# Seven products for eight in three block pairs of a decoder's FFN input product

## The chip, the cores and the metric

One Trainium2 chip, one of its cores. The metric is the device time of one execution in microseconds (us); lower is better. Of several runs the median counts.

## What is computed

Two decoder layers over 256 tokens of width 1024, all in float32. A layer has a combined input projection, a sparse and a differential attention, gated up projections and an output projection; then comes the feed forward, which the change is about:

```
h = rms_norm(x, ffn_norm)
gate, up = jnp.split(h @ w_ffn_in, 2, axis=-1)      # 1024 -> 2 x 2816
x = x + (jax.nn.silu(gate) * up) @ w_ffn_out        # 2816 -> 1024
```

## The kernel before, in words

Every float32 operand of a dense product is split into a high part, rounded to the type that TensorE multiplies in one pass, and the low rest. `mm3` (lines 170 to 174) makes three matmuls of each product: high x high, high x low (of the weight), low (of the activation) x high. The activations (128 tokens x 128 of K) are the stationary operand, up to 512 columns of weights the moving one.

Weights come in units of 1 MB, 512 of K x 512 columns (or 256 of K x 1024 for the output product), in the order of `unit_order` (lines 55 to 69). A unit is loaded in two halves of 128x1024 into a ring of eight buffers (`load_half`, line 112, tag `raw`, issued on SyncE's queue) and split half by half (`split_half`): ScalarE copies the high part (line 135), VectorE subtracts for the low part (line 136). High and low parts lie in rings of four units (tags `wh`, `wl`), so that a unit's split waits until the product of the unit four places ahead is done.

TensorE and GpSimd keep the order in which the program is written. That of VectorE, ScalarE and the loads is found by a planner. `tick` counts blocks of TensorE's work, and `later` sets steps to run some ticks on.

The feed forward (lines 785 to 852) has eleven slabs of 256 gate and 256 up columns. `slab(s, t)` makes the input product of token tile t with one slab: 8 blocks of K x 3 matmuls of 512 columns into one bank of PSUM, from two units (`fi`). `fi_fin` (line 792) applies Silu on ScalarE (line 794), multiplies by up on VectorE (line 795), and three ticks later transposes the hidden tile and splits it (`hilo`, lines 212 and 213). `fo_part` (line 807) makes the output product of a slab's hidden tiles, 6 matmuls per token tile and half of the columns, into four banks (`facc`) that are held through the feed forward (line 813); the eight banks of PSUM share one tag (line 97). From slab 1 on the output product of the slab before follows each slab; those of the last three (`TAIL`) stand at the end, token tile by token tile. Between them the next layer's norm begins: sum (line 819), square (line 230), reciprocal root on GpSimd (lines 208 and 209), scaling (line 242), transposes (`norm_T`, line 244).

Before the feed forward the norm of the first token tile is transposed ahead of the last block of the output projection (line 772), that of the second in the middle of `slab(1, 0)` (line 825).

Of the kernel before, what the change touches and what calls it, by code (L numbers as in the profile page):

```python
# [10 lines left out]
F32 = mybir.dt.float32  # L11
# [3 lines left out]
ALU = mybir.AluOpType  # L15
# [10 lines left out]
TAIL = 3  # L26
# [16 lines left out]
RAWS = 8  # L43
# [5 lines left out]
MT_AT, FI_AT = 3, 3  # L49
WO = ((0, 0, 0), (0, 1, 0), (0, 0, 1), (1, 0, 0), (1, 1, 0), (0, 1, 1), (1, 0, 1), (1, 1, 1))  # L50
FRONT = ("gA0", "ix")
# [3 lines left out]
def unit_order():  # L55
    o = []

    def blk(n):
        o.extend([(n, 0), (n, 1)])

    for n in FRONT + BLOCKS:
        blk(n)
    o.extend([("wo", i) for i in range(4)])
    for s in range(NFO):
        blk(f"fi{s}")
        if 0 < s <= NFO - TAIL:
            o.append(("fo", s - 1))
    o.extend([("fo", s) for s in range(NFO - TAIL, NFO)])
    return o
# [3 lines left out]
PACKED = [u for u in ORDER if u[0] != "ix"]  # L73
# [3 lines left out]
def tile_trunk(ctx, tc, x, positions, wpk, widx, gnorm, gbias, gqk, dlam, subln, const, invf, out):  # L77
# [22 lines left out]
    seq, uidx = [], {}  # L100
    for l in range(DEPTH):
        n = 0
        for nm in ORDER:
            uidx[(l,) + nm] = len(seq)
            if nm[0] == "ix":
                seq.append((widx[l, nm[1]], 2 * IDXW))
            else:
                seq.append((wpk[l, n], 1024))
                n += 1
    ready, raws, loaded, split = [], {}, [0], [0]  # L110

    def load_half():
        n = loaded[0]
        loaded[0] += 1
        i, j = divmod(n, 2)
        src, w = seq[i]
        raws[n] = wp.tile([P, 1024], F32, name=f"raw{i}{j}", tag="raw", bufs=RAWS)[:, :w]
        nc.sync.dma_start(raws[n], src[j])

    def split_half(parts=1, between=None):  # L120
        n = split[0]
        split[0] += 1
        i, j = divmod(n, 2)
        w = seq[i][1]
        if j == 0:
            ready.append([wp.tile([P, 2048], F32R, name=f"w{h}{i}", tag="w" + h, bufs=RING) for h in "hl"])
        hi, lo = ready[i]
        if n not in raws:
            load_half()
        raw = raws.pop(n)  # L130
        m = w // parts
        for k in range(parts):
            c = slice(j * w + k * m, j * w + (k + 1) * m)
            piece = raw[:, k * m:(k + 1) * m]
            nc.scalar.activation(hi[:, c], piece, AF.Copy)  # L135
            nc.vector.tensor_tensor(lo[:, c], piece, hi[:, c].bitcast(F32), ALU.subtract)  # L136
            if k == 0 and between:
                between()
# [4 lines left out]

    def unit(l, name, i, kc, w):
# [25 lines left out]
    def mm3(acc, stat, mov, first, last):  # L170
        (sh, sl), (mh, ml) = stat, mov
        nc.tensor.matmul(acc, lhsT=sh, rhs=mh, start=first, stop=False)  # L172
        nc.tensor.matmul(acc, lhsT=sh, rhs=ml, start=False, stop=False)  # L173
        nc.tensor.matmul(acc, lhsT=sl, rhs=mh, start=False, stop=last)  # L174
# [40 lines left out]
    def heads(v, n):  # L215
        return v.rearrange("p (h d) -> p h d", h=n)
# [27 lines left out]
    def norm_T(N, t, *gs):  # L244
        for g in gs or range(2):
            b = bank(f"{N['name']}T{t}{g}")
            transposes(b, N["h"][t, g], range(4))
            hilo(*[a[:, 4 * g:4 * g + 4, t * P:(t + 1) * P] for a in N["T"]], heads(b, 4))

# [21 lines left out]
    for _ in range(8):  # L271
        load_half()
# [390 lines left out]
    for l in range(DEPTH):  # L663
# [34 lines left out]
        def y_tiles(n):  # L698
            return [pp.tile([P, 4, S], F32R, name=f"{n}{h}{l}", tag="yT", bufs=2) for h in "hl"]
# [91 lines left out]

        def fi_fin(s, t, acc):
# [4 lines left out]
            def fin():  # L797
                b = bank(f"aTT{l}{s}{t}")
                transposes(b, g, range(2, 4))
                a = t2k([P, 2, 2, P], f"aT{l}{s}{t}", F32R)  # L800
                hilo(a[:, 0], a[:, 1], heads(b[:, :S], 2))
                aT[s, t] = a
            later(FI_AT, fin)
# [3 lines left out]
        def fo_part(s, t, c, a=0, b=512):  # L807
# [6 lines left out]
            for kc in range(2):  # L814
                mm3(facc[t, c][:, a:b], [aT[s, t][:, j, kc] for j in range(2)],
                    [w[:, kc, 512 * c + a:512 * c + b] for w in W], first and kc == 0, end and kc == 1)
# [38 lines left out]
def pack(w_in, w_up_a, w_up_b, w_out, w_ffn_in, w_ffn_out):  # L855
# [8 lines left out]
    for l in range(DEPTH):  # L864
        for h in range(2):
            widx[l, h] = lay(w_in[l, 512 * h:512 * h + 512, IDX:IDX + IDXW])
        for n, (name, i) in enumerate(PACKED):
# [4 lines left out]
            elif name == "wo":  # L872
                c, k = divmod(i, 2)
                w = w_out[l, 512 * k:512 * k + 512, 512 * c:512 * c + 512]
            elif name.startswith("fi"):
# [40 lines left out]
```

## Time and profile before

| | |
|---|---|
| median of 3 runs | 781.02 us (780.72 to 781.04) |
| profiled execution | span 778.8 us; no other time of its own is shown |
| TensorE busy | 769.7 us (99%), 3718 instructions, transposes among them |
| VectorE busy | 502.6 us (65%) |
| ScalarE busy | 422.6 us (54%) |
| GpSimd busy | 80.5 us (10%) |
| moved by DMA | 137.83 MB, mean 177 GB/s |
| first layer's feed forward | from 207.4 us of the span on |

The span runs from the first to the last instruction. PE is TensorE, PEld its weight loads, DVE VectorE, ACT ScalarE, POOL GpSimd, SPq the queue of SyncE. Matmuls overlap, so that a busy time of PE says that it never stood idle, not that it ran at its peak. A wait is idle time of an engine with the line that it waited at and the instruction that ended the wait. The granted clock is that of TensorE, 1.00 being full speed.

### The profile page before, as it was taken

To read this page: it belongs to the slowest core of one execution; us is meant where nothing else is said; L and a number is where in the kernel's file an instruction comes from. 1 tells how busy PE (TensorE), PEld (TensorE's weight loads), DVE (VectorE), ACT (ScalarE), POOL (GpSimd) and SP (SyncE) were. 2 spreads that over 40 slices of the span, in tenths; PEclk is the share of its full clock that TensorE was granted. 3 is DMA by queue.
4 is the path that set the end of the run, shared out by engine and by line. 5 is a ranking of instruction groups with operands and counts; after the bars stand their busy time and mean duration, and the time that the engine had idled before them with its cause. 6 is when DMAs were issued, how large, how long until landed. Compare 5 with 4: busy or idle time off the path is not lost.

```text
span 778.8 us, 10446 instructions
## 1 busy us (share of the span) xinstructions
PE 769.7 (99%) x3718; PEld 631.6 (81%) x3718; DVE 502.6 (65%) x907; ACT 422.6 (54%) x922; POOL 80.5 (10%) x103
## 2 busy tenths in 40 slices
PE   8999999999999999999999999999999999999998
PEld 5877888888888888888888788788888888888887
DVE  4899767777764544455478986677766644554541
ACT  5776687565553433443357585876645534444440
POOL 6541220010110000000011310200001000000000
PEclk9999999999999999999999999999999999999999
DMA  8855645356546655556456365534564754566501
GB/s 290 298 170 172 220 159 176 113 162 202 193 149 227 204 189 189 162 186 197 146 176 216 124 202 152 187 122 151 187 189 163 242 189 163 179 199 204 175 0 55
DMA packets 41013, 137.83 MB, mean 177 GB/s; under 512 B 5201, under 2 KB 5969, under 8 KB 40962
## 3 DMA queue, kind: packets, MB, share of 16 engines
q1 hardware_dynamic: 40880, 136.97, 53.5%
q8 instruction: 29, 0.48, 0.2%
q0 software_dynamic: 80, 0.20, 0.1%
q14 instruction: 22, 0.18, 0.1%
q10 hardware_dynamic: 2, 0.00, 0.0%
HBM read 136.11 MB, written 1.05 MB: 176 GB/s over the span
## 4 chain that ended last, share of the span: by engine, by line
PE 88%; DVE 4%; ACT 3%; DMA 2%; POOL 1%; issue 1%; SPq 0%; ACTq 0%; DVEq 0%
PE fi L174 10%; PE fi L173 10%; PE fi L172 10%; PE fo L174 5%; PE fo L173 5%; PE fo L172 5%; PE gB L172 2%; PE gB L174 2%; PE wo L174 2%; PE wo L172 2%; PE gB L173 2%; PE wo L173 2%; PE gA L172 1%; DMA raw<-wpk 1%; PE gA L174 1%; PE gA L173 1%
## 5 line engine op out<-in xcount | busy, mean ns | idle before, releaser
L136 DVE TENSOR_TENSOR wl<-raw,wh 128x1024 fp32r<-128x1024 f32 (+2 forms) x254 | 299.4, 1205 | 129.5 <-ACT wh L135 128.7
L135 ACT ACTIVATE wh<-raw 128x1024 fp32r<-128x1024 f32 (+2 forms) x254 | 255.2, 1044 | 138.8 <-PE fo L174 50.0
L172 PE MATMUL fo<-wh,aT 128*128 128x512 f32 (+1 forms) x182 | 71.4, 392 | 0.0
L174 PE MATMUL fo<-wh,aT 128*128 128x512 f32 (+1 forms) x182 | 69.7, 383 | 0.0
L173 PE MATMUL fo<-wl,aT 128*128 128x512 f32 (+1 forms) x182 | 69.7, 383 | 0.0
L172 PE MATMUL fi<-wh,f0Th 128*128 128x512 f32 x176 | 69.6, 395 | 0.0
L172 PE MATMUL fi<-wh,f1Th 128*128 128x512 f32 x176 | 69.6, 395 | 0.0
L174 PE MATMUL fi<-wh,f1Tl 128*128 128x512 f32 x176 | 68.7, 390 | 0.0
L174 PE MATMUL fi<-wh,f0Tl 128*128 128x512 f32 x176 | 68.7, 390 | 0.0
L173 PE MATMUL fi<-wl,f0Th 128*128 128x512 f32 x176 | 68.6, 390 | 0.0
L173 PE MATMUL fi<-wl,f1Th 128*128 128x512 f32 x176 | 68.6, 390 | 0.0
L794 ACT ACTIVATE sg<-fi 128x256 f32<-128x256 f32 x44 | 16.9, 384 | 83.5 <-PE fi L174 83.5
L795 DVE TENSOR_TENSOR sg<-sg,fi 128x256 f32<-128x256 f32 x44 | 18.4, 418 | 43.5 <-ACT sg L794 43.5
L174 PEld LDWEIGHTS fo<-wh,aT 128*128 128x128 f32 x182 | 34.2, 188 | 6.7
L173 PEld LDWEIGHTS fo<-wl,aT 128*128 128x128 f32 x182 | 34.3, 188 | 6.0
L172 PEld LDWEIGHTS fo<-wh,aT 128*128 128x128 f32 x182 | 34.2, 188 | 6.0
L174 PEld LDWEIGHTS fi<-wh,f0Tl 128*128 128x128 f32 x176 | 33.0, 188 | 6.9
L174 PEld LDWEIGHTS fi<-wh,f1Tl 128*128 128x128 f32 x176 | 33.0, 188 | 6.9
L173 PEld LDWEIGHTS fi<-wl,f1Th 128*128 128x128 f32 x176 | 33.1, 188 | 6.5
L173 PEld LDWEIGHTS fi<-wl,f0Th 128*128 128x128 f32 x176 | 33.1, 188 | 6.5
L172 PEld LDWEIGHTS fi<-wh,f1Th 128*128 128x128 f32 x176 | 33.0, 188 | 6.5
L172 PEld LDWEIGHTS fi<-wh,f0Th 128*128 128x128 f32 x176 | 33.0, 188 | 6.5
(880 smaller groups left out, 1548.7 us busy)
## 6 DMA issues: line engine op xcount, KB each, us to landing
raw<-wpk SPq DMA_DIRECT2D x244, 512.0 KB, 4.4
raw<-widx SPq DMA_DIRECT2D x8, 324.0 KB, 6.8
x<-x SPq DMA_DIRECT2D x4, 256.0 KB, 3.7
gf<-gnorm SPq DMA_DIRECT2D x4, 256.0 KB, 5.7
out<-x SPq DMA_DIRECT2D x3, 256.0 KB, 2.0
ga<-gnorm SPq DMA_DIRECT2D x2, 256.0 KB, 4.3
gq<-gqk SPq DMA_DIRECT2D x2, 160.0 KB, 6.3
dl<-dlam SPq DMA_DIRECT2D x2, 128.0 KB, 5.1
```

The source lines that it names most:

```text
L135: nc.scalar.activation(hi[:, c], piece, AF.Copy)
L136: nc.vector.tensor_tensor(lo[:, c], piece, hi[:, c].bitcast(F32), ALU.subtract)
L172: nc.tensor.matmul(acc, lhsT=sh, rhs=mh, start=first, stop=False)
L173: nc.tensor.matmul(acc, lhsT=sh, rhs=ml, start=False, stop=False)
L174: nc.tensor.matmul(acc, lhsT=sl, rhs=mh, start=False, stop=last)
L794: nc.scalar.activation(g[:, :S], acc[:, :S], AF.Silu)
L795: nc.vector.tensor_tensor(g[:, S:], g[:, :S], acc[:, S:], ALU.mult)
```

## The change

Three pairs of slabs (3 and 4, 6 and 7, 9 and 10) get another input product. A pair has 512 gate and 512 up columns and K in two halves, so its weights are four units: 11 and 21 for gate (first and second half of K), 12 and 22 for up. Eight products of 128 tokens with one unit would be needed; token tile 0 and 1 have A11, A12 and A21, A22 as halves of K. Instead there are seven, with T1 = 12 - 11, T2 = 22 - T1, T3 = 22 - 12, T4 = 21 - T2 on the weights and S1 = A21 + A22, S2 = S1 - A11, S3 = A11 - A21, S4 = A12 - S2 on the activations: X = A11 x 11, Y = A12 x 21, V = S4 x 22, X += S2 x T2, Z = S3 x T3, X += S1 x T1, Z += A22 x T4. The gate of tile 0 is X + Y, its up X + V at the end; tile 1 has the later sums of X and Z.

The differences are made on VectorE, in the buffer of one of their operands (T1 in that of 11, T3 in that of 12, T4 in that of T2) but for T2, which has one of its own; 22 is loaded into the buffer of the attention outputs (tag `yT`). The splits are instructions of 128x2048 on VectorE, and on ScalarE for the T's. The sums S are made once per layer (`quarter_sums`) from the transposed norm. Loading buffers are four of 128x2048, in place of eight of 128x1024; a unit's two loads go to one buffer.

In the feed forward VectorE and ScalarE keep the written order now: behind product i come the high part of unit i+4, the low part of unit i+3 and the difference that unit i+5 needs. Dense slabs (0, 1, 2, 5, 8) use a unit for both token tiles, one after the other, before the next unit. The tail has two slabs. Core of the diff:

```diff
@@ -23,7 +23,7 @@
-TAIL = 3
+TAIL = 2
...
-RAWS = 8
+RAWS = 4
...
+QUAD_AT = (3, 3)
...
+FFN = (("D", 2), ("Q", 3), ("D", 5), ("Q", 6), ("D", 8), ("Q", 9))
+LOOK = 4
+PRODUCTS = ("11", "21", "22", "fo", "T2", "T3", "T1", "fo", "T4")
+LOADED = {"11": "11", "T1": "12", "21": "21", "22": "22"}
...
-    for s in range(NFO):
-        blk(f"fi{s}")
-        if 0 < s <= NFO - TAIL:
-            o.append(("fo", s - 1))
-    o.extend([("fo", s) for s in range(NFO - TAIL, NFO)])
+    blk("fi0")
+    blk("fi1")
+    done = 0
+    for kind, s in FFN:
+        for n in PRODUCTS if kind == "Q" else (0, 1, "fo") if done else (0, 1):
+            o.append((n, done) if n == "fo" else (("fi" if kind == "D" else "q") + str(s), n))
+            done += n == "fo"
+    o.extend([("fo", s) for s in range(done, NFO)])
...
+    def raw_of(u):
+        if u not in held:
+            src, w = where[u]
+            name = "raw" + "".join(str(a) for a in u)
+            if u[2] == "22":
+                raw = pp.tile([P, 2048], F32, name=name, tag="yT", bufs=1)
+            else:
+                raw = wp.tile([P, 2048], F32, name=name, tag="raw", bufs=RAWS)[:, :2 * w]
+            for j in range(2):
+                nc.sync.dma_start(raw[:, j * w:j * w + w], src[j])
+            held[u] = raw
+        return held[u]
...
+    def difference(n):
+        l, name, i = seq[n]
+        if n + 1 < len(seq) and seq[n + 1][2] == "T2":
+            l, name, i = seq[n + 1][:2] + ("T1",)
+        elif name[0] != "q" or i == "T1":
+            return
+        D = diffs.setdefault((l, name), {})
+        def less(new, a, b, to=None):
+            a, b = [D[x] if x[0] == "T" else raw_of((l, name, x)) for x in (a, b)]
+            to = {"a": a, "b": b}[to] if to else b8([P, 2048], f"T2{l}{name}")
+            nc.vector.tensor_tensor(to, a, b, ALU.subtract)
+            D[new] = to
+        if i == "T1":
+            less("T1", "12", "11", "b")
+        elif i == "T2":
+            less("T2", "22", "T1")
+        elif i == "T3":
+            less("T3", "22", "12", "b")
+        elif i == "T4":
+            less("T4", "21", "T2", "b")
+    def high(n):
+        u = seq[n]
+        raw = diffs[u[:2]].pop(u[2]) if u[2] in ("T1", "T3", "T4") else diffs[u[:2]]["T2"] if u[2] == "T2" else raw_of(u)
+        hi = new_ready(n)[0]
+        m = 1 if u[1][0] == "q" and u[2][0] == "T" else 2
+        w = 2048 // m
+        for k in range(m):
+            nc.scalar.activation(hi[:, k * w:k * w + w], raw[:, k * w:k * w + w], AF.Copy)
+        if u[2] == "11":
+            raw_of(u[:2] + ("21",)), raw_of(u[:2] + ("12",))
+        stage["raw", n] = raw
+    def low(n):
+        nc.vector.tensor_tensor(ready[n][1], stage.pop(("raw", n)), ready[n][0].bitcast(F32), ALU.subtract)
+        split[0] += 2
+    def staged(k, end):
+        for fn, m in ((high, k), (low, k - 1), (difference, k + 1)):
+            n = max(stage.get(fn, 0), split[0] // 2)
+            while n <= min(m, end):
+                fn(n)
+                n += 1
+            stage[fn] = n
...
+    def quarter_sums(N, banks):
+        name = N["name"]
+        f1, f2 = N["f"]
+        tiles = [b8([P, 4, 4, P], f"{name}S{h}", F32R) for h in "hl"]
+        N["S"] = [[a[:, i] for a in tiles] for i in range(4)]
+        s1, s2, s3, s4 = [t2k([P, 512], f"{name}s{i}") for i in range(4)]
+        nc.scalar.activation(s4, banks[1], AF.Copy)
+        nc.vector.tensor_tensor(s1, banks[0], s4, ALU.add)
+        nc.vector.tensor_tensor(s3, f1, banks[0], ALU.subtract)
+        nc.vector.tensor_tensor(s2, s1, f1, ALU.subtract)
+        nc.vector.tensor_tensor(s4, f2, s2, ALU.subtract)
+        for i, v in ((0, s1), (3, s4), (1, s2), (2, s3)):
+            hilo(*N["S"][i], heads(v, 4))
...
-                norm_T(NF, 0)
+                keep_quarters(NF, norm_T(NF, 0))
...
+        def ahead(name, i):
+            staged(uidx[l, name, i] + LOOK, uidx[l, "fo", NFO - 1])
+        def fo_all():
+            s = fo_next[0]
+            fo_next[0] += 1
+            for t in range(NT):
+                for c in range(2):
+                    fo_part(s, t, c)
+                tick()
+                if t == 0:
+                    ahead("fo", s)
+        def dense(s):
+            acc = [bank(f"fi{s}{l}{t}") for t in range(NT)]
+            for half in range(2):
+                for t in range(NT):
+                    by_tok(acc[t], fT, t, unit(l, f"fi{s}", half, 4, 512), 4 * half, 4, half == 0, half == 1)
+                    if half == 1:
+                        fi_fin(s, t, acc[t])
+                    tick()
+                ahead(f"fi{s}", half)
+        def quad(s):
+            name = f"{l}{s}"
+            def A(t, g):
+                return [a[:, 4 * g:4 * g + 4, t * P:(t + 1) * P] for a in fT]
+            S1, S2, S3, S4 = NF["S"]
+            def product(acc, stat, n, first, fins=()):
+                W = unit(l, f"q{s}", n, 4, 512)
+                for kc in range(4):
+                    mm3(acc, [a[:, kc, :] for a in stat], [w[:, kc, :] for w in W],
+                        first and kc == 0, kc == 3, not first)
+                for fin in fins:
+                    fin()
+                tick()
+                ahead(f"q{s}", n)
+            G, U = [[t2k([P, 512], f"{n}{t}{name}") for t in range(NT)] for n in "gu"]
+            def copied(to, p):
+                return lambda: nc.scalar.activation(to, p, AF.Copy)
+            def plus(to, p):
+                return lambda: nc.vector.tensor_tensor(to, to, p, ALU.add)
+            def added(to, a, p):
+                return lambda: nc.vector.tensor_tensor(to, a, p, ALU.add)
+            def silu(t):
+                return lambda: nc.scalar.activation(G[t], G[t], AF.Silu)
+            def gated(t):
+                def f():
+                    nc.vector.tensor_tensor(U[t], G[t], U[t], ALU.mult)
+                    later(QUAD_AT[t], lambda: hidden_T(s, t, U[t], range(4)))
+                return f
+            X = bank(f"qX{name}")
+            product(X, A(0, 0), "11", True, [copied(G[0], X)])
+            Y = bank(f"qY{name}")
+            product(Y, A(0, 1), "21", True, [plus(G[0], Y), silu(0)])
+            V = bank(f"qV{name}")
+            product(V, S4, "22", True)
+            fo_all()
+            product(X, S2, "T2", False, [copied(G[1], X)])
+            Z = bank(f"qZ{name}")
+            product(Z, S3, "T3", True)
+            product(X, S1, "T1", False, [copied(U[1], X), added(U[0], U[1], V), gated(0), plus(U[1], Z)])
+            fo_all()
+            product(Z, A(1, 1), "T4", False, [plus(G[1], Z), silu(1), gated(1)])
         slab(0, 0)
-        slab(1, 0, mid=lambda: norm_T(NF, 1))
-        for s in range(NFO):
-            for t in range(NT):
-                if s > 1 or t:
-                    slab(s, t)
-            if 0 < s <= NFO - TAIL:
-                for t in range(NT):
-                    for c in range(2):
-                        fo_part(s - 1, t, c)
-                    tick()
+        slab(1, 0, mid=lambda: quarter_sums(NF, norm_T(NF, 1)))
+        with tc.manual_schedule(engines={mybir.EngineType.DVE, mybir.EngineType.Activation}):
+            for i in range(2):
+                slab(i, 1, mid=lambda: ahead(f"fi{i}", 0))
+                ahead(f"fi{i}", 1)
+            for kind, s in FFN:
+                if kind == "Q":
+                    quad(s)
+                else:
+                    dense(s)
+                    if fo_next[0]:
+                        fo_all()
+            fo_all()
```

Not shown: the dictionary of loads by unit, `keep_quarters` (two ScalarE copies of A11 and A12's banks), `hidden_T` (transposes and splits two hidden blocks for a dense slab, four for a pair), and the packing of units 11, 12, 21, 22.

## Rows read from the trace of the kernel before

**Rows 1.** The page's head, engines' busy time, and the chain that ended last.

```profile
span 778.8 us, 10446 instructions
PE 769.7 (99%) x3718; PEld 631.6 (81%) x3718; DVE 502.6 (65%) x907; ACT 422.6 (54%) x922; POOL 80.5 (10%) x103
...
PE 88%; DVE 4%; ACT 3%; DMA 2%; POOL 1%; issue 1%; SPq 0%; ACTq 0%; DVEq 0%
```

**Rows 2.** Waits of PE: us in total, times, longest.

```profile
PE a0T L181 <- DVE a0h L242: 1.6, 1, 1.6
PE warm L279 <- DVE idle L274: 1.4, 1, 1.4
PE aq10T L181 <- DVE aq10q L367: 0.8, 1, 0.8
...
```

**Rows 3.** Busy time by stretch, the middle of layer 0's feed forward.

```profile
core 0: us, PE busy (x) PEld busy (x) DVE busy (x) ACT busy (x) POOL busy (x), PEclk, DMA share, GB/s
...
231.00:376.00 145.00, 145.00 (x657) 119.55 (x656) 73.34 (x88) 62.74 (x88) 0.00 (x0) 1.00 0.58 190
```

**Rows 4.** Timeline, PE in an output product and a hidden tile's transposes: start, duration.

```profile
300.03 0.39 PE L172 MATMUL fo<-wh,aT 128*128 128x512 f32 x1
...
303.20 0.39 PE L174 MATMUL fo<-wh,aT 128*128 128x512 f32 x1
...
303.44 0.38 PE L181 MATMUL aTT<-cst,sg 128*128 128x128 f32 x2
...
303.89 0.39 PE L173 MATMUL fi<-wl,f0Th 128*128 128x512 f32 x1
```

**Rows 5.** Groups by line and shape, VectorE's splits: busy us, mean ns.

```profile
L136 DVE TENSOR_TENSOR wl<-raw,wh 128x1024 fp32r<-128x1024 f32 x242 | 290.4, 1225 | 127.3 <-ACT wh L135 126.6
...
L136 DVE TENSOR_TENSOR wl<-raw,wh 128x648 fp32r<-128x648 f32 x8 | 6.3, 828 | 1.2 <-ACT wh L135 1.2
```

**Rows 6.** Timeline, DVE and ACT around the feed forward's start.

```profile
182.75 0.68 DVE L213 TENSOR_TENSOR mTl<-mT,mTh 128x512 fp32r<-128x512 f32 x1
183.35 1.22 DVE L136 TENSOR_TENSOR wl<-raw,wh 128x1024 fp32r<-128x1024 f32 x1
...
203.03 3.49 DVE L136 TENSOR_TENSOR wl<-raw,wh 128x1024 fp32r<-128x1024 f32 x3
...
223.38 2.36 DVE L136 TENSOR_TENSOR wl<-raw,wh 128x1024 fp32r<-128x1024 f32 x2 [2.88 <-ACT wh L135]
...
207.55 2.01 ACT L135 ACTIVATE wh<-raw 128x1024 fp32r<-128x1024 f32 x2 [0.64 <-PE wo L174]
```

**Rows 7.** Timeline, a slab's end handed from PE to ACT to DVE.

```profile
308.90 0.39 PE L174 MATMUL fi<-wh,f0Tl 128*128 128x512 f32 x1
...
309.32 0.38 ACT L794 ACTIVATE sg<-fi 128x256 f32<-128x256 f32 x1 [3.41 <-PE fi L174]
...
309.74 0.42 DVE L795 TENSOR_TENSOR sg<-sg,fi 128x256 f32<-128x256 f32 x1 [2.32 <-ACT sg L794]
```

**Rows 8.** Loads in 231 to 376 us: rate in 40 slices, landing, SPq's waits.

```profile
GB/s 269 374 268 131 75 257 250 271 23 163 276 234 198 8 279 292 181 113 131 238 220 269 14 197 293 211 167 15 285 283 205 86 139 268 199 262 7 220 251 1
...
DMA to landing us min/median/max: 3.1/4.2/6.0
...
SPq L118 <- DVE wl L136: 82.7, 34, 6.5
```

**Rows 9.** Timeline, the next layer's norm at the end of layer 0.

```profile
384.98 0.69 DVE L819 TENSOR_TENSOR x<-x,fo 128x512 f32<-128x512 f32 x1 [3.40 <-PE fo L174]
...
386.97 0.57 POOL L209 TENSOR_TENSOR a1r<-a1r,mhalf 128x1 f32<-128x1 f32 x1
...
387.58 1.42 DVE L242 SCALAR_TENSOR_TENSOR a1h<-x,a1r,ga 128x512 f32<-128x512 f32 x2 [1.54 <-POOL a1r L209]
...
390.48 1.03 PE L181 MATMUL a1T<-cst,a1h 128*128 128x128 f32 x8
```

More of the change, by code (lines that the diff above doesn't have):

```diff
@@ L97, in bank, with new_ready @@
         return ps.tile([P, 512], F32, name=name, tag="ps", bufs=8)
-    seq, uidx = [], {}
+    seq, uidx, where = [], {}, {}
     for l in range(DEPTH):
[L102 to L106, printed above, removed]
-            else:
[L108 to L118, printed above, removed]
+        for n, u in enumerate(PACKED):
+            where[(l,) + u] = (wpk[l, n], 1024)
+        for j in range(2):
+            where[l, "ix", j] = (widx[l, j], 2 * IDXW)
+        for u in ORDER:
+            uidx[(l,) + u] = len(seq)
+            seq.append((l,) + u)
+    held, ready, split = {}, [], [0]
+    def raw_of(u):
[4 more added lines that the diff above has]
+                raw = pp.tile([P, 2048], F32, name=name, tag="yT", bufs=1)
+            else:
+                raw = wp.tile([P, 2048], F32, name=name, tag="raw", bufs=RAWS)[:, :2 * w]
+            for j in range(2):
+                nc.sync.dma_start(raw[:, j * w:j * w + w], src[j])
+            held[u] = raw
+        return held[u]
+    def new_ready(i):
+        assert len(ready) == i
+        ready.append([wp.tile([P, 2048], F32R, name=f"w{h}{i}", tag="w" + h, bufs=RING) for h in "hl"])
+        return ready[i]
     def split_half(parts=1, between=None):
@@ L123, in split_half @@
         i, j = divmod(n, 2)
[L124 to L130, printed above, removed]
+        hi, lo = ready[i] if j else new_ready(i)
+        raw = raw_of(seq[i])
+        w = raw.shape[-1] // 2
         m = w // parts
@@ L168, in thread, with mm3 @@
             later(start + i, s)
-    def mm3(acc, stat, mov, first, last):
+    def mm3(acc, stat, mov, first, last, more=False):
         (sh, sl), (mh, ml) = stat, mov
-        nc.tensor.matmul(acc, lhsT=sh, rhs=mh, start=first, stop=False)
-        nc.tensor.matmul(acc, lhsT=sh, rhs=ml, start=False, stop=False)
-        nc.tensor.matmul(acc, lhsT=sl, rhs=mh, start=False, stop=last)
+        nc.tensor.matmul(acc, lhsT=sh, rhs=mh, start=first, stop=False, skip_group_check=more)
+        nc.tensor.matmul(acc, lhsT=sh, rhs=ml, start=False, stop=False, skip_group_check=more)
+        nc.tensor.matmul(acc, lhsT=sl, rhs=mh, start=False, stop=last, skip_group_check=more)
     def tok(xT, kc, t):
@@ L244, in norm_T @@
     def norm_T(N, t, *gs):
+        banks = []
         for g in gs or range(2):
@@ L248, in norm_T, with keep_quarters @@
             hilo(*[a[:, 4 * g:4 * g + 4, t * P:(t + 1) * P] for a in N["T"]], heads(b, 4))
+            banks.append(b)
+        return banks
+    def keep_quarters(N, banks):
+        N["f"] = [t2k([P, 512], f"{N['name']}f{g}") for g in range(2)]
+        for f, b in zip(N["f"], banks):
+            nc.scalar.activation(f, b, AF.Copy)
+    def quarter_sums(N, banks):
[11 more added lines that the diff above has]
+            hilo(*N["S"][i], heads(v, 4))
     def consts_in(l):
@@ L270, in tile_trunk @@
     nc.sync.dma_start(ivf, invf.to_broadcast([P, 32]))
-    for _ in range(8):
-        load_half()
+    for n in range(4):
+        raw_of(seq[n])
     idle = t2k([P, 512], "idle")
@@ L698, in y_tiles @@
         def y_tiles(n):
-            return [pp.tile([P, 4, S], F32R, name=f"{n}{h}{l}", tag="yT", bufs=2) for h in "hl"]
+            both = pp.tile([P, 2, 4, S], F32R, name=f"{n}{l}", tag="yT", bufs=1)
+            return [both[:, i] for i in range(2)]
         def up_a(c, t, acc):
@@ L790, in tile_trunk, with hidden_T @@
         facc = {}
+        def hidden_T(s, t, g, chunks):
+            b = bank(f"aTT{l}{s}{t}")
+            transposes(b, g, chunks)
+            n = len(chunks)
+            w = n * P
+            if n == 2:
+                a = t2k([P, 512], f"aT{l}{s}{t}", F32R)
+                parts = [a[:, :w], a[:, w:]]
+            else:
+                parts = [t2k([P, 512], f"aT{h}{l}{s}{t}", F32R) for h in "hl"]
+            parts = [heads(a, n) for a in parts]
+            hilo(*parts, heads(b[:, :w], n))
+            for k in range(n // 2):
+                aT[s + k, t] = [a[:, 2 * k:2 * k + 2] for a in parts]
         def fi_fin(s, t, acc):
@@ L795, in fi_fin @@
             nc.vector.tensor_tensor(g[:, S:], g[:, :S], acc[:, S:], ALU.mult)
[L797 to L803, printed above, removed]
+            later(FI_AT, lambda: hidden_T(s, t, g, range(2, 4)))
         last = l + 1 == DEPTH
```

16 lines of the change are left out of this document (11 added, 5 removed).

## The prediction

> **What bounds the kernel now.** I read the head of the profile's page first [rows 1]: TensorE is busy for 769.7 of 778.8 us, and the chain that ended last runs through it for 88% of the span. The waits of TensorE come next [rows 2]: the reader is to see that the longest is 1.6 us; the list has eight entries, 5.7 us in all, and none of them is of the feed forward. The busy time by stage [rows 3] says the same: in each stretch of the feed forward TensorE is busy for the whole stretch, at a granted clock of 1.00, with VectorE at 73.3 of 145.0 us. So the feed forward lasts as long as its matmuls, and a matmul that goes is time that goes, as long as its operands still come in time.
>
> What one matmul is worth is not its "mean ns", since matmuls overlap. From the start at 300.03 to that at 303.20 there are 14 steps, 0.2264 us each, while a single one is shown with 0.39 [rows 4]. Twelve, one product of a token tile with half of K, take 2.72 us. Two transposes move the next matmuls by 0.23.
>
> No row gives the profiled execution a time of its own beside its span; the median of the runs, 781.02, lies 2.2 us above it, and I add these 2.2 at the end. A difference of 0.2%, 1.6 us, is about what a measurement of this kernel can tell from none.
>
> **What is removed.** A pair of slabs is 96 matmuls (two token tiles, two halves of K, two slabs of 12), and becomes seven products of 12, that is 84. Three pairs in each of two layers: 72 x 0.2264 = **16.3 us less** on the engine that sets the end. The output products, the transposes of the hidden tiles (four per token tile and pair, in one group now) and the bytes loaded (four 1 MB units per pair) stay.
>
> **What is added on VectorE.** A pair now splits seven units, not four, and makes four differences. Each is one instruction of 128x2048. The trace has none, so I go by its slope: 1225 ns at 1024 and 828 at 648 [rows 5] give 1.056 ns per column, hence 2.31 us. Instructions in an unbroken run start closer than they last: two of 1024 take 2.36 together, three 3.49, and a 512 is followed after 0.60 though shown with 0.68 [rows 6]. So one takes 2.2 us of the engine. A period of one dense slab and one pair with three output products is then 16 of these (12 splits, 4 differences), 35.2 us; eight instructions of 512 (six that join the products, two for hidden tiles), 4.8; four of 256, 1.3: 41.3 us. TensorE has 204 matmuls and 12 transposes in it, 47.5 us. VectorE goes from half busy to 87%, in an order that is now fixed. ScalarE has 12 splits of 1.9 (two of 1024 take 2.01 [rows 6]) and some 4.5 us of copies, Silu and hidden tiles: 27 of 47.5, so it hides.
>
> **Inside a pair.** I walked the three engines through the new order with these durations, 0.2 us from TensorE to ScalarE (the slab's last matmul starts at 308.90, frees the engine one step later, at 309.13, and Silu starts at 309.32) and 0.04 from ScalarE to VectorE [rows 7]; for VectorE to TensorE I take 0.2 from the same rows. Times count from the first slab. In the first pair, product 11 starts at 34.4 (twelve times 2.72, and 16 transposes at 0.11), and T2 could start at 48.4 (three products, four transposes and an output product of 24 matmuls later). VectorE's row in that time: split of 21 from 29.9, difference T1 from 32.1, the dense slab's two gate products until 35.3, split of 22 until 37.5, difference T2 until 39.7, a hidden tile, split of output unit 0 until 42.2, difference T3 until 44.4, the joining of the first two products until 45.0; then it waits 1.1 us for a hidden tile that ScalarE holds back behind the Silu of the joined gate, and splits T2 until 48.6. With the hand-over TensorE waits 0.5. VectorE then runs without a break: splits of T3 and T1, the difference for T4, and the split of output unit 1 until 57.4, where TensorE wants it at 57.1: 0.6 more. In the second and third pair an output product lies ahead of product 11, and the same split is ready 0.45 us before it is wanted. So the cost is 1.1 us per layer, **2.2 us**; bounds are 0, if the engine is as little in the way as rows 3 have it now, and 3.4 per layer if every instruction holds VectorE for its full 2.31. I take the walk, as rows 6 show the shorter step.
>
> The Trainium skill, VectorE: DVE Perf Modes, section The DRAIN you can't avoid, says that the next instruction does not start until the pipe of the one before has emptied, a start-to-start gap of the whole duration, and that only an instruction which is not held starts earlier. Were each one held, the pairs would cost 3.4 us per layer and the sum would end at 772.9. Rows 6 disagree for runs of like instructions, 1.13 apart at 1.225.
>
> **Loads.** The four loading buffers hold whole units now, and during a pair three of them are kept long (11 and 12, which become T1 and T3, and 21 until T4's difference), so that output units go through the fourth. A half unit lands 3.1 to 6.0 us after its issue, and the queue moves up to 293 GB/s over a slice, once 374 [rows 8]; I take 6 us for a unit, and 3.5 to 4 us apart in a burst. If the buffer that comes free first is used, output unit 1 is issued at 42.2 and is there at 48.5, and ScalarE turns to it at 49.7: nothing is lost. At 4 us per unit the walk gives 0.2 us more per layer, at 4.5 it gives 6.4. The loading queue waits for VectorE's splits already [rows 8], so it is the split that sets when a load starts.
>
> **Start of the feed forward.** The quarter sums put four sums and four splits of 512 on VectorE (8 x 0.60 = 4.8 us) and seven copies of 0.5 on ScalarE (two of these copy the first token tile's quarters), around the second token tile's transposes. VectorE has a gap of 2.9 us there and starts the third slab's split at 223.4 [rows 6]; it would be at 225 to 228, and that slab starts at 230.6. Cost nothing; with the gap gone and the split late by its own 2.2 us it would be 2 us per layer.
>
> **End of the first layer's feed forward.** With two slabs in the tail, not three, the next norm's first transposes stand earlier. The chain there is the sum at 384.98, a square, GpSimd's power at 386.97, the scaling from 387.58 for 1.42, the transposes at 390.48 [rows 9]. Six matmuls fewer in each of two groups bring the transposes 2.7 us forward, to 387.7, where the second scaled half is ready at 389.0 plus the hand-over: **1.5 us** lost, once (0 to 3, if a split of 2.01 comes ahead of the square on ScalarE).
>
> **Attention.** Loads of whole units start up to one half's split later than now, 1.2 us, against three more units in the ring: nothing, with -1 to 2 us, since the order that is found for VectorE and ScalarE there may change.
>
> Sum: 778.8 - 16.3 + 2.2 + 1.5 = 766.2, and with the 2.2 around the span **768.4 us**.
>
> **The rivals.**
> 1. *VectorE sets the pace in the pairs.* Each split that waits for ScalarE holds the engine for its full 2.31 us. All three pairs then stall, 3.4 us per layer: 772.9. For it: a margin of 0.45 us, and 87% busy in a fixed order. Against: rows 6. 0.22.
> 2. *A starved output unit; slower than before.* If output unit 1 gets the buffer of 12, free only after T3's split at 50.8, it lands at 57.1. ScalarE has its split in line ahead of the copy that frees the bank X for T1, so TensorE waits 5.6 us ahead of T1 in the first pair and 4.4 in each other: 14.9 per layer in place of 1.1, 27.5 more, 796. It decides where the unit lands more than about 2 us after ScalarE turns to it. Loads 5 us apart would cost as much in the walk, 14 to 15 per layer. Against it: the queue's best slices [rows 8] and that four of the eight banks of PSUM are held through the feed forward (line 813) while the others go round, so buffers are not handed out in turn. 0.15.
> 3. *Transfers at 4.5 us per unit*, 6.4 us more per layer: 781, no difference. 0.05.
> 4. *All covers hold*, with no wait in the pairs and at the norm: 778.8 - 16.3 + 2.2 = 764.7. For it: that no wait stands in rows 2. 0.10.
>
> **How the numbers follow.** The forecast itself has 0.48, and is the likeliest: 768.4. Faster by over 0.2% are it and rivals 1 and 4, 0.80; rival 3 is the same, 0.05; rival 2 slower, 0.15. The range reaches from 763.5, rival 4 with 1 us gained in attention, to 781, which takes in rival 3 and the upper bounds of the small terms with rival 1, and leaves out rival 2.
>
> **What would show it.** Right: TensorE's feed-forward matmuls 984, not 1056; VectorE instructions of 128x2048 near 2.3 us, and VectorE near 87% busy between pairs; TensorE's waits of about half a microsecond on the splits of T2 and of the second output unit in the first pair of each layer, and one of 1 to 2 us on the scaled tile at the layer's end. Wrong: waits of several microseconds ahead of T1 with ScalarE behind a load (rival 2), waits in every pair on VectorE (rival 1), or TensorE idle in attention, where I put nothing.

## The result and the profile after

The changed kernel took 766.95 us (median of four runs, 765.97 to 767.07 but for one disturbed run, which the ratio leaves out; 766.82 without it), the kernel before 780.87 (780.03 to 781.04): a ratio of 0.9819 [0.9801, 0.9837], 14 us or 1.8% faster. The prediction of 768.4 was 1.5 us too high, and its forecast case is the one that came.

The head of the page after, with the busy times and the chain that ended last, stands against [rows 1]:

```profile
span 764.2 us, 10201 instructions
PE 753.3 (99%) x3640; PEld 617.4 (81%) x3640; DVE 610.9 (80%) x907; ACT 469.7 (61%) x942; POOL 78.2 (10%) x103
PE 84%; DVE 8%; issue 2%; ACT 2%; DMA 1%; POOL 1%; SPq 0%; DVEq 0%; ACTq 0%
```

TensorE is still busy for 99% of a span that is 14.6 us shorter. VectorE gained 108 us of work and has twice its share of the chain, but the time went down with TensorE's instructions. By line, the feed forward's input matmuls are 984 (480 of dense slabs, 504 of the seven products) where they were 1056. The whole trace has 78 instructions of TensorE fewer: these 72, and six more because the shorter tail has fewer output matmuls of half width at the end.

TensorE's waits (engine, line waited at, releaser: us in total, times, longest), against [rows 2]:

```profile
PE a1T L245 <- DVE a1h L306: 1.0, 1, 1.0
...
PE fo L237 <- DVE wl L197: 0.7, 2, 0.3
```

Two entries are new, the ones forecast: the scaled tile at the end of the first layer's feed forward (`a1T`) and an output unit's split in the first pair of each layer (`fo`). In the feed forward there is none for T2, though one of half a microsecond was among the signs named for the forecast, and none on ScalarE or a load.

Busy time by stretch, the middle of layer 0's feed forward and a part of it between pairs (columns as in [rows 3]):

```profile
232.00:380.00 148.00, 147.65 (x668) 121.45 (x667) 130.98 (x90) 86.87 (x97) 0.00 (x0) 1.00 0.52 192
280.00:330.00 50.00, 50.00 (x228) 41.32 (x227) 44.35 (x30) 30.45 (x34) 0.00 (x0) 1.00 0.55 206
```

VectorE, 73.3 of 145.0 us before, is at 88% to 89% (87% was worked out), and TensorE stands still for 0.35 us of 148.

To see where the time came from I took the start of the first matmul of each stage from the two timelines:

| stretch | before | after | measured | by the prediction |
|---|---|---|---|---|
| up to the first feed forward | 207.4 | 206.7 | -0.7 | 0 |
| feed forward of layer 0 | 186.7 | 181.2 | -5.5 | -8.15 + 1.1 + 1.5 = -5.6 |
| second layer up to its feed forward | 195.0 | 194.0 | -1.0 | 0 |
| feed forward of layer 1 | 185.9 | 178.5 | -7.4 | -8.15 + 1.1 = -7.1 |
| last output sums | 3.8 | 3.8 | 0 | 0 |

So the sum is right almost as it stands, in the stages that it is about; which of its terms are off inside them is worked out further down. The 2.0 us by which the span fell below the predicted 766.2 are mostly from the two stretches where I put nothing.

### The profile page after: what moved, and what is told of

It is laid out like the page before. It is cut to its first block, busy times and chain, and to the rows that moved or that the text cites. A ratio compares the mean times of both kernels' runs of the same rounds, so it can differ in the third digit from the quotient of the medians.

```text
span 764.2 us, 10201 instructions
## 1 busy us (share of the span) xinstructions
PE 753.3 (99%) x3640; PEld 617.4 (81%) x3640; DVE 610.9 (80%) x907; ACT 469.7 (61%) x942; POOL 78.2 (10%) x103
## 4 chain that ended last, share of the span: by engine, by line
PE 84%; DVE 8%; issue 2%; ACT 2%; DMA 1%; POOL 1%; SPq 0%; DVEq 0%; ACTq 0%
PE fo L237 5%; PE fo L238 5%; PE fo L236 5%; PE fi L238 4%; PE fi L236 4%; PE fi L237 4%; DVE wl L197 2%; PE gB L236 2%; PE gB L238 2%; PE gB L237 2%; PE gA L236 2%; PE gA L237 2%; PE gA L238 2%; PE wo L238 2%; PE wo L237 2%
## 5 line engine op out<-in xcount | busy, mean ns | idle before, releaser
L236 PE MATMUL fo<-wh,aTh 128*128 128x512 f32 (+1 forms) x100 | 38.3, 383 | 0.0
L238 PE MATMUL fo<-wh,aTl 128*128 128x512 f32 (+1 forms) x100 | 38.1, 381 | 0.0
L237 PE MATMUL fo<-wl,aTh 128*128 128x512 f32 (+1 forms) x100 | 38.1, 381 | 0.0
L236 PE MATMUL fi<-wh,f0Th 128*128 128x512 f32 x80 | 31.8, 398 | 0.0
L236 PE MATMUL fi<-wh,f1Th 128*128 128x512 f32 x80 | 31.7, 397 | 0.0
L236 PE MATMUL fo<-wh,aT 128*128 128x512 f32 x80 | 31.5, 394 | 0.0
L238 PE MATMUL fo<-wh,aT 128*128 128x512 f32 x80 | 31.2, 391 | 0.0
L238 PE MATMUL fi<-wh,f1Tl 128*128 128x512 f32 x80 | 31.2, 390 | 0.0
L238 PE MATMUL fi<-wh,f0Tl 128*128 128x512 f32 x80 | 31.2, 390 | 0.0
L237 PE MATMUL fi<-wl,f1Th 128*128 128x512 f32 x80 | 31.2, 390 | 0.0
L237 PE MATMUL fi<-wl,f0Th 128*128 128x512 f32 x80 | 31.1, 389 | 0.0
```

## The experiments

### How many pairs: none, two, four back to back

My theory: what the change gives is TensorE's matmuls, 24 fewer per pair of both layers (5.4 us), as long as VectorE has room. Rivals: the gain comes from the new order, the whole-unit splits or the shorter tail; and VectorE's room does not matter.

All slabs dense, in the new order with the new splits and the tail of two:

```diff
-FFN = (("D", 2), ("Q", 3), ("D", 5), ("Q", 6), ("D", 8), ("Q", 9))
+FFN = tuple(("D", s) for s in range(2, 11))
...
-        for n in PRODUCTS if kind == "Q" else (0, 1, "fo") if done else (0, 1):
+        for n in PRODUCTS if kind == "Q" else (0, 1, "fo") if done or s > 2 else (0, 1):
...
-                    if fo_next[0]:
+                    if fo_next[0] or s > 2:
```

> All eleven slabs dense, in the new order of VectorE and ScalarE, with the new loads, the quarter sums and the two-slab tail left in. Theory 1 (TensorE's matmuls set the time, 0.2264 us each): the 72 matmuls come back, 16.3 us, and the waits inside the pairs go, 1.0 us, so 766.9 + 15.3 = 782 us, within 1.5; feed-forward input matmuls 1056. Rival (the new order, the unit loads or the tail made the gain, not the products): the time stays below 777. Rival (the new order costs, and the products gain more than 16.3): above 785.

Measured: 782.59 us, 1.0031 [1.0017, 1.0044]. Everything of the change but the pairs gives nothing; it costs 1.8 us. In the trace 1.6 us of it are in the first layer's feed forward (188.3 us for 186.7), and most of that is the norm at its end, which the shorter tail brings with it: the transposes start 1.0 us late (`a1T`, 0.8 in the list of waits) and last 1.29 us, not 1.03 [rows 9].

Two pairs:

```diff
-FFN = (("D", 2), ("Q", 3), ("D", 5), ("Q", 6), ("D", 8), ("Q", 9))
+FFN = (("D", 2), ("Q", 3), ("D", 5), ("Q", 6), ("D", 8), ("D", 9), ("D", 10))
```

> Two pairs per layer, slabs 9 and 10 dense. Theory 1 (each pair is worth 12 matmuls per layer, 2.7 us, less what its waits cost, which only the first has): 5.4 us more than the changed kernel, 772.3 us (771 to 773.5). Rival (the gain sits in the first pairs, as the last one leads into the tail): 768 or less.

Measured: 772.43 us, 0.9894 [0.9874, 0.9915]. From none to two pairs 10.2 us, from two to three 5.5: each pair is worth 5.1 to 5.5 us, and 24 matmuls at 0.2264 [rows 4] are 5.4.

Four pairs, one behind the other with no dense slab between:

```diff
-FFN = (("D", 2), ("Q", 3), ("D", 5), ("Q", 6), ("D", 8), ("Q", 9))
+FFN = (("D", 2), ("Q", 3), ("Q", 5), ("Q", 7), ("Q", 9))
```

> Four pairs back to back behind one dense slab (slab 2, then 3 and 4, 5 and 6, 7 and 8, 9 and 10). Theory 1 (a pair with two output products has 30 us of TensorE but about 35 of VectorE, so VectorE becomes the bound where no dense slab follows): waits of 1.4 to 1.7 us ahead of several products of each later pair, 18 us more per layer, 800 us or above (790 to 815). Rival (the seven products are worth 2.7 us per pair and layer wherever they stand): 761.5.

Measured: 789.52 us, 1.0117 [1.0098, 1.0136]: slower than the kernel before, though 24 more matmuls are gone. The direction was right, the size too large. TensorE's waits, and the busy times of the stretch:

```profile
PE fo L237 <- DVE wl L197: 10.9, 14, 1.4
PE qX L237 <- DVE wl L197: 6.7, 6, 1.1
PE qV L237 <- DVE wl L197: 4.7, 6, 0.8
```

```profile
232.00:400.00 168.00, 156.07 (x691) 124.36 (x690) 153.50 (x105) 96.84 (x108) 0.87 (x2) 1.00 0.49 184
282.00:318.00 36.00, 32.37 (x142) 25.58 (x142) 34.06 (x22) 20.82 (x21) 0.00 (x0) 1.00 0.46 175
```

These are the waits in every later pair that rival 1 of the prediction has: 26 on VectorE, TensorE idle for 11.9 of 168 us, VectorE busy at 91%. The run changes two things at once, the number of pairs and the dense slabs between them, and its timeline tells them apart: the first pair, right behind a dense slab as before, has only the output unit's wait of 0.3 us, while each of the three that stand behind another pair has 3.6 us in four waits, with VectorE busy for 34.06 of 36.00 us (the second line is such a stretch). A pair makes seven splits and four differences, and the dense slab behind it is where VectorE catches up. The alternation is a condition of the gain: without it and with the fourth pair, 5.4 us of matmuls are gone and the time is 22.6 us longer.

### VectorE's work: the differences left out, one split doubled

The four differences are not computed, so that the T's are split from other tiles; everything else stays:

```diff
-            to = {"a": a, "b": b}[to] if to else b8([P, 2048], f"T2{l}{name}")
-            nc.vector.tensor_tensor(to, a, b, ALU.subtract)
-            D[new] = to
+            D[new] = {"a": a, "b": b}[to] if to else a
```

> The four differences of each pair are left out (24 VectorE instructions of 2.2 us), the products use the undifferenced units, so this part of the input product is not computed. Theory 1 (VectorE is hidden but for the first pair's waits): 0.5 to 1.5 us faster, 766 us; VectorE near 560 us busy. Rival (VectorE sets the pace in the pairs): 4 us or more faster, 763 or less.

Measured: 765.56 us, 0.9812 [0.9795, 0.9829]. 24 instructions of 2.2 us are gone from VectorE, 53 us of work, and the time falls by 1.4 (0.5 by the ratios, whose intervals overlap). With no difference to make, TensorE has no wait in the pairs, and the two feed forwards of its trace last 180.4 and 177.6 us, where the changed kernel's last 181.2 and 178.5: what the waits cost there is some 0.9 us per layer.

The split of T3 made twice:

```diff
-        nc.vector.tensor_tensor(ready[n][1], stage.pop(("raw", n)), ready[n][0].bitcast(F32), ALU.subtract)
+        raw = stage.pop(("raw", n))
+        for _ in range(2 if seq[n][2] == "T3" else 1):
+            nc.vector.tensor_tensor(ready[n][1], raw, ready[n][0].bitcast(F32), ALU.subtract)
```

> VectorE makes the split of T3 twice in each pair, 2.2 us more right behind product 22. Theory 1 (fully hidden only as far as a margin of 0.5 us; walk of the three engines): 2.8 us of waits in the first pair of a layer and 0.9 in each other, 4.0 per layer more than now, 775 us (772 to 777). Rival (VectorE at 80% has room): 767 to 768. Rival (VectorE is the pace): all of it, 13.2 us more, 780.

Measured: 777.64 us, 0.9958 [0.9945, 0.997], 10.7 us above the changed kernel and slightly beyond the range given. The waits of the run:

```profile
PE fo L239 <- DVE wl L199: 5.2, 6, 0.9
PE qZ L239 <- DVE wl L199: 3.0, 2, 1.5
```

Six more instructions occupy VectorE for 6 x 2.2 = 13.2 us, and 10.7 of these reach the end of the kernel. Taking 53 us of work away is worth 1 to 2; adding 13.2 costs 10.7. The kernel stands at the edge where VectorE's order is as long as TensorE's.

### The lead of the splits

Splits and differences one product later:

```diff
-LOOK = 4
+LOOK = 3
```

> High parts three units ahead, not four, low parts two, differences four. Theory 1 (what counts is the lead of the split over the product, not the average load): product 22 and output unit 0 of the first pair wait 1.8 and 3.7 us, output unit 0 of the other pairs 1.7 each, 8 us more per layer, 783 us (778 to 787). Rival (only the average load of VectorE counts): no change, 766 to 768.

Measured: 786.44 us, 1.008 [1.0065, 1.0095], with the same work on every engine. Waits, then TensorE's timeline behind the longest (start, us, instruction), then the busy time of the two stretches:

```profile
PE fo L237 <- DVE wl L197: 12.7, 6, 3.4
PE qV L237 <- DVE wl L197: 3.0, 2, 1.5
```

```profile
257.78 0.50 PE L237 MATMUL fo<-wl,aT 128*128 128x512 f32 x1 [3.40 <-DVE wl L197]
...
259.40 0.63 PE L237 MATMUL fo<-wl,aT 128*128 128x512 f32 x1
259.82 0.63 PE L238 MATMUL fo<-wh,aT 128*128 128x512 f32 x1
...
262.69 0.39 PE L236 MATMUL fo<-wh,aT 128*128 128x512 f32 x1
262.92 0.40 PE L237 MATMUL fo<-wl,aT 128*128 128x512 f32 x1
```

```profile
254.00:262.70 8.70, 5.30 (x17) 3.89 (x16) 7.73 (x6) 5.38 (x5) 0.00 (x0) 0.80 0.43 161
262.70:270.00 7.30, 7.30 (x34) 6.00 (x33) 6.04 (x3) 3.33 (x4) 0.00 (x0) 1.00 0.86 330
```

The waits are 15.7 us, 15 more than in the changed kernel, of a span 20.7 longer. A part of the rest is TensorE's clock: after standing idle for 3.40 us the steps are 0.42 us from 259.4 on, the 1.2 GHz level, and 0.23 again, the 2.4 GHz level, from 262.7; the granted clock of the first stretch is 0.80. None of the waits of 0.3 us in the changed kernel does this, and a long wait does not always: behind the like wait of 3.39 us in the second layer the steps stay at 0.23 us, at a granted clock of 1.00 from 645 to 650 us. How late a split may be is thus as much a part of the change as how many there are.

### A difference on GpSimd

GpSimd is idle in the feed forward [rows 3], so one might give it T4's difference:

```diff
-            nc.vector.tensor_tensor(to, a, b, ALU.subtract)
+            (nc.gpsimd if new == "T4" else nc.vector).tensor_tensor(to, a, b, ALU.subtract)
```

> T4's difference on GpSimd instead of VectorE. Theory 1 (the remaining waits in the pairs come from VectorE's run of four splits and this difference ahead of output unit 1): the two waits of 0.5 us go, 766 us. Rival (GpSimd takes 5 us or more for 128x2048, by its 1.02 us for 128x320, and ScalarE's split of T4 waits for it with the copies behind it): 768 to 775. Rival (the two engines slow each other): VectorE's 128x2048 take longer than 2.29 us while GpSimd's runs.

Measured: 788.48 us, 1.0093 [1.007, 1.0116]. The last rival holds, that the two engines slow each other; the time lies far beyond the 768 to 775 of the other. The timeline of VectorE and GpSimd in the first pair, then in the second:

```profile
253.96 2.28 DVE L197 TENSOR_TENSOR wl<-T20q,wh 128x2048 fp32r<-128x2048 f32 x1
256.15 8.88 DVE L197 TENSOR_TENSOR wl<-raw0q,wh 128x2048 fp32r<-128x2048 f32 x2
256.46 6.43 POOL L172 TENSOR_TENSOR T20q<-raw0q,T20q 128x2048 f32<-128x2048 f32 x1 [36.53 <-PE fo L238]
...
308.41 4.63 POOL L172 TENSOR_TENSOR T20q<-raw0q,T20q 128x2048 f32<-128x2048 f32 x1 [45.53 <-DVE wl L197]
308.58 6.62 DVE L197 TENSOR_TENSOR wl<-raw0q,wh 128x2048 fp32r<-128x2048 f32 x1 [0.30 <-ACT wh L191]
```

The same two splits take 4.49 us together in the changed kernel (shown further down, for the first pair). The 4.39 more are about what GpSimd needs after 258.4, where VectorE's first split would end by itself: 262.89 - 258.4 = 4.5. In the second pair GpSimd is first: it ends at 313.04, and VectorE's split, shown from 308.58, ends 2.16 us later, about the time of one split. So the two do not run beside each other: one difference taken from VectorE, 2.2 us, costs it 4.4. The Trainium skill, SBUF — State Buffer, section Who interferes with whom, has the rule: an instruction of VectorE with two inputs in SBUF contends with one of GpSimd that reads SBUF, and the ports that they share are an exclusive lock. Both pairs agree with it.

The blocking alone is not the whole loss. The profiled execution is 24.0 us longer than the changed kernel's. TensorE waits 14.3 us for low parts (`qZ` 8.2, `qX` 6.1), where the changed kernel has 0.7. Its 3640 instructions, as many as in the changed kernel, keep it busy for 764.5 us, not 753.3: behind five of the six waits, of 2.0 to 3.1 us, it is on its 1.2 GHz level for a while (granted clock 0.50 from 265 to 270 us, 0.83 from 310 to 320). That part had no place in the expectation.

### Loads of whole units

The four buffers of whole units, in the kernel before:

```diff
-RAWS = 8
+RAWS = 4
...
-        raws[n] = wp.tile([P, 1024], F32, name=f"raw{i}{j}", tag="raw", bufs=RAWS)[:, :w]
+        if j == 0:
+            whole[i] = wp.tile([P, 2048], F32, name=f"raw{i}", tag="raw", bufs=RAWS)[:, :2 * w]
+        raws[n] = whole[i][:, j * w:j * w + w]
```

> The kernel before, with only the loading buffers changed to four whole units. Theory 1 (the 1.7 us that attention was shorter in the one profile have nothing to do with the loads; the first 0.7 come from when TensorE's matmul steps change from 0.43 to 0.23 us, which differs from run to run): 780.8 us, the same within 0.8. Rival (loads of whole units make attention faster): 779.1.

Measured: 780.62 us, 1.0 [0.9989, 1.0011]. The buffers cost and give nothing by themselves, and so do not explain the microsecond that the second layer's attention lost: from its first matmul to its feed forward it takes 194.7 us here, 195.0 before and 194.0 after.

### The waits that are left

Layer 0 with a tail of three slabs, as before the change, to cover the norm:

```diff
-            fo_all()
+            if last:
+                fo_all()
+        tail = TAIL if last else TAIL + 1
...
-                    for s in range(NFO - TAIL, NFO):
+                    for s in range(NFO - tail, NFO):
```

> Three slabs in the tail of the first layer, as before the change, two in the last. Theory 1 (the wait ahead of the next norm's transposes comes from the shorter tail): that wait, 1.0 us and 0.4 inside the transposes, is gone, 765.5 us, and nothing else moves. Rival (the wait moves to the first block of the next layer): 767.

Measured: 766.61 us, 0.9822 [0.9804, 0.9841], no different from the changed kernel. The wait at `a1T` is gone, but there is another at the last output unit, whose split now lies behind the joining of the last pair in VectorE's written order:

```profile
369.80 0.69 DVE L980 TENSOR_TENSOR u<-g,u 128x512 f32<-128x512 f32 x1 [0.93 <-ACT g L976]
370.41 2.29 DVE L197 TENSOR_TENSOR wl<-raw0fo,wh 128x2048 fp32r<-128x2048 f32 x1
...
372.75 0.50 PE L237 MATMUL fo<-wl,aTh 128*128 128x512 f32 x1 [1.66 <-DVE wl L197]
```

The gain was there and was given back 10 us earlier, a case that neither theory had.

The Silu of the joined gate one product later, so that ScalarE has the hidden tile ready before it:

```diff
-            product(Y, A(0, 1), "21", True, [plus(G[0], Y), silu(0)])
+            product(Y, A(0, 1), "21", True, [plus(G[0], Y)])
...
-            product(V, S4, "22", True)
+            product(V, S4, "22", True, [silu(0)])
```

> Only the Silu of the joined gate is one product later on ScalarE, so that the hidden tile's copy comes ahead of it. Theory 1 (VectorE's wait of 1 us for that tile is what makes the first pair's split late): VectorE's wait before the split of T2 is gone and so are TensorE's two waits on output unit 1; 766.0 us, 1 less than the changed kernel. Rival (the two differences between the dense slab's gates make it late all the same): the waits stay.

Measured: 764.79 us, 0.9799 [0.9779, 0.9819]. The waits at the output units are gone, and with them 2.2 us of the median (1.6 by the ratios, whose intervals overlap). In the trace the feed forwards are 1.2 and 0.9 us shorter (180.0 and 177.6 us), 0.3 of it at the norm's transposes; that is about twice what was expected.

Both together, and the last output unit's split put ahead of the joining of the last pair:

```diff
+                if (s, n) == (9, "T4"):
+                    ahead(f"q{s}", n)
                 for fin in fins:
                     fin()
```

> Three slabs in the first layer's tail, the last output unit's split ahead of the last pair's joining on VectorE, and the Silu of the joined gate one product later on ScalarE. Theory 1 (the remaining waits come from the order of single instructions): no wait ahead of the next norm's transposes, none of 1.7 us on the last output unit, none of 0.5 in the first pairs; 2.5 us faster than the changed kernel, 764.4 us (763.5 to 765.5). Rival (a wait turns up at the next place in the chain): 766 to 767.

Measured: **763.4 us**, 0.978 [0.9761, 0.9798], the fastest kernel of the study, 0.1 below the range expected. Its interval is the only one that lies clear below the changed kernel's [0.9801, 0.9837]. All of TensorE's waits in it, and VectorE's timeline at the two places:

```profile
PE warm L366 <- DVE idle L361: 1.4, 1, 1.4
PE a0T L245 <- DVE a0h L306: 1.2, 2, 0.6
PE ix01T L245 <- DVE ix01q L493: 0.8, 1, 0.8
PE aq10T L245 <- DVE aq10q L454: 0.8, 1, 0.8
PE gA L236 <- ACT a0Th L709: 0.5, 1, 0.5
PE bk10T L245 <- DVE bk10q L454: 0.2, 1, 0.2
```

```profile
252.00 0.42 DVE L277 TENSOR_TENSOR aT<-aTT,aT 128x256 fp32r<-128x256 f32 x1
252.34 2.28 DVE L197 TENSOR_TENSOR wl<-T20q,wh 128x2048 fp32r<-128x2048 f32 x1
...
367.81 2.28 DVE L197 TENSOR_TENSOR wl<-raw0fo,wh 128x2048 fp32r<-128x2048 f32 x1
```

No wait of the feed forward is left in the list. The split of T2 starts at 252.34 (253.63 in the changed kernel), the last output unit's at 367.81 (370.41 with the longer tail alone).

## Why the prediction was right, and where its terms were off

**What is removed**: right. There are 72 input matmuls fewer in the trace, and the runs with none, two and three pairs price a pair at 5.1 to 5.5 us against 5.4.

**What is added on VectorE**: right. The groups by shape give the duration that the slope of [rows 5] gave as 2.31:

```profile
L197 DVE TENSOR_TENSOR wl<-raw0q,wh 128x2048 fp32r<-128x2048 f32 x15 | 34.0, 2284 | 0.6 <-ACT wh L191 0.6
...
L172 DVE TENSOR_TENSOR raw0q<-raw0q,raw0q 128x2048 f32<-128x2048 f32 x6 | 13.7, 2284 | 0.0
```

**Inside a pair**: the places were right, the price of T2 was too high. VectorE and ScalarE in the first pair of layer 0, around the split of T2:

```profile
247.24 2.28 DVE L197 TENSOR_TENSOR wl<-raw0fo,wh 128x2048 fp32r<-128x2048 f32 x1
249.44 2.28 DVE L172 TENSOR_TENSOR raw0q<-raw0q,raw0q 128x2048 f32<-128x2048 f32 x1
251.64 0.68 DVE L970 TENSOR_TENSOR g<-g,qY 128x512 f32<-128x512 f32 x1
253.29 0.43 DVE L277 TENSOR_TENSOR aT<-aTT,aT 128x256 fp32r<-128x256 f32 x1 [0.97 <-ACT aT L276]
253.63 2.28 DVE L197 TENSOR_TENSOR wl<-T20q,wh 128x2048 fp32r<-128x2048 f32 x1
255.83 4.49 DVE L197 TENSOR_TENSOR wl<-raw0q,wh 128x2048 fp32r<-128x2048 f32 x2
...
262.44 2.28 DVE L197 TENSOR_TENSOR wl<-raw0fo,wh 128x2048 fp32r<-128x2048 f32 x1
```

```profile
252.35 0.63 ACT L976 ACTIVATE g<-g 128x512 f32<-128x512 f32 x1 [3.35 <-DVE g L970]
252.89 0.37 ACT L276 ACTIVATE aT<-aTT 128x256 fp32r<-128x256 f32 x1
```

The order is that of the walk: VectorE waits 0.97 us (1.1 predicted) for a hidden tile that ScalarE holds behind the Silu, then splits T2 until 255.91. TensorE in the same place, at T2 and at the output unit:

```profile
255.67 0.39 PE L236 MATMUL qX<-wh,f0Sh 128*128 128x512 f32 x1
255.97 0.50 PE L237 MATMUL qX<-wl,f0Sh 128*128 128x512 f32 x1
256.30 0.39 PE L238 MATMUL qX<-wh,f0Sl 128*128 128x512 f32 x1
...
264.04 0.39 PE L236 MATMUL fo<-wh,aT 128*128 128x512 f32 x1
264.77 0.50 PE L237 MATMUL fo<-wl,aT 128*128 128x512 f32 x1 [0.35 <-DVE wl L197]
265.11 0.40 PE L238 MATMUL fo<-wh,aT 128*128 128x512 f32 x1
```

The step that failed is the one that let TensorE wait for the split when the product *starts*, with a hand-over of 0.2. The first of the three matmuls takes the high part, which ScalarE made long before; only the second takes VectorE's low part, one step of 0.23 later. It starts 0.06 us after the split's shown end. So TensorE lost 0.07 us at T2 (a step of 0.30) and 0.5 at the output unit (0.73), and 0.1 more in the step behind each (0.33 and 0.34): 0.2 at T2, not the 0.5 predicted, and 0.6 at the output unit, as predicted. The second agrees in part by luck: TensorE, which had lost less at T2, came to the output unit earlier, while the split there was as late as VectorE's unbroken run makes it. The steps of layer 1 come to the same 0.8 us, and the run without differences puts it at 0.9. So the pairs cost 1.6 to 1.8 us in the two layers, not 2.2.

**The rule that was weighed, and rival 1.** The splits at 253.63 and 255.83 and the two instructions at 247.24 and 249.44 start 2.20 us apart at 2.28 shown, in runs of like instructions. The Trainium skill, VectorE: DVE Perf Modes, section The DRAIN you can't avoid, would have the next instruction start after the whole duration, and an instruction that is not held earlier; the trace shows the second of these. That the margin was thin is shown too: the doubled split and the four pairs bring waits like those of rival 1, but through more work for VectorE. In both runs its splits still start 2.20 us apart.

**Loads, and rival 2**: nothing, as predicted. Output unit 1 was issued by 250.0 us and a unit's landing takes 3.2 to 5.5 us in this stretch, so it is there by 255.5; ScalarE turns to it at 256.76, without a wait, as the walk had it (1.2 us in hand). A starved output unit was not tried: T1, T3 and 21 hold three of the four buffers, so there is none to take away. Its price, 27.5 us, stays an estimate.

**Start of the feed forward**: the sums and their splits fill VectorE from 219.08 to 223.9, and the third slab's split starts at 225.71 (225 to 228 predicted), in time. A wait of 0.25 us of TensorE for slab 0's hidden tile at 223.9 was not predicted.

**End of the first layer's feed forward**: right. GpSimd, VectorE and TensorE, against [rows 9]:

```profile
382.53 0.57 POOL L273 TENSOR_TENSOR a1r<-a1r,mhalf 128x1 f32<-128x1 f32 x1
...
383.13 1.41 DVE L306 SCALAR_TENSOR_TENSOR a1h<-x,a1r,ga 128x512 f32<-128x512 f32 x2 [2.18 <-POOL a1r L273]
383.94 1.38 PE L245 MATMUL a1T<-cst,a1h 128*128 128x128 f32 x8 [0.99 <-DVE a1h L306]
```

The last output matmul starts at 382.56 and its step ends at 382.79; the transposes start 1.15 later and last 1.38 instead of 1.03 [rows 9], together 1.5 us, the predicted 1.5. The best version wins it back: there the eight transposes take 1.03 us, with no wait ahead of them.

**Attention**: put at nothing, it gave 1.7 us. The 0.7 of the first layer is no effect of the change: its feed forward starts at 205.7 to 208.3 us over the eleven experiments, and TensorE's steps go from 0.43 to 0.23 us at 15.8 us of the span before, 13.9 after, and between 12.7 (where the feed forward starts at 205.7) and 16.9 in the experiments. The 1.0 of the second layer is one: the kernels with pairs take 193.9 to 194.2 us for this stretch, those with none 194.7 (all dense; whole-unit loads) and 195.0. The planner finds another order for VectorE and ScalarE there, and a wait of 0.5 us at an attention matmul of the kernel before is not in the list after; that this is the cause is argued, not shown.

In sum, against the predicted span of 766.2: attention 1.7 less, the pairs 0.4 less (by the run without differences), the matmuls 0.3 less (a step with its surroundings is 0.230, which makes 16.6 of 16.3) and the hidden tile 0.25 more, 764.1 where 764.2 was measured. Inside the feed forwards the errors are small and partly cancel; most of the 1.5 us by which the forecast was off is the attention that it put at nothing.

## What to carry to other kernels

Trading a matmul for work on another engine pays at the price of the matmul's step as long as that engine's written order is no longer than TensorE's over a period: work out that period and place a stretch with slack (here a dense slab) behind each dense stretch of extra work. Before counting a wait, ask which instruction of the consumer needs the late operand: a product whose first matmul takes the early half has a step in hand. When one wait is covered, look at what moves up in its place, as with the longer tail, and move the two together.

## What was not expected of the hardware

- VectorE and GpSimd with 128x2048 differences of SBUF tiles went one after the other: 8.88 us for two splits that take 4.49 without the difference beside them. The idle engine was no help: 788.5 us against 767.0, a part of it through TensorE's clock.
- A wait of 3.40 us amid the kernel put TensorE on its 1.2 GHz level for 3 to 4 us behind it; five of the six waits of 2.0 to 3.1 us in the run with GpSimd put it there too, for 3 to 6 us. One of 3.39 and one of 2.04 us did not, and none of the waits of 0.3 to 1.7 us in the feed forwards did.
- At the start of the kernel the rise to the 2.4 GHz level comes at 12.7 to 16.9 us, differently by run; the first feed forward starts between 205.7 and 208.3 us.
